# A hybrid decoder trunk on one core: another order of the seven products in the w_up blocks, and a first tile that is loaded beside its weights

## The chip, the cores and the metric

The kernel runs on one core of one Trainium2 chip. The metric is device time in microseconds (us) of one execution, as the median over runs; smaller is better. TensorE (PE) multiplies, VectorE (DVE), ScalarE (ACT) and GpSimd (POOL) work elementwise, and SyncE (SP) issues most of the loads.

## The reference, cut to what matters

The computation is a decoder trunk of two layers on 512 tokens of width 1024. Each layer is a mixer (attention and a Mamba-2 scan side by side) and a SwiGLU feed-forward, each behind an RMSNorm and added to the residual. What the change touches is the first input projection and the feed-forward:

```python
D_MODEL, SEQ, DEPTH = 1024, 512, 2
FFN_HIDDEN = ((8 * D_MODEL + 3 * 256 - 1) // (3 * 256)) * 256    # 2816

def rmsnorm(x, w):
    y = x * lax.rsqrt(jnp.mean(x * x, axis=-1, keepdims=True) + EPS)
    return y * w

def swiglu(h, w_gate, w_up, w_down):
    return (jax.nn.silu(h @ w_gate) * (h @ w_up)) @ w_down

def reference(x, ...):
    h = x
    for layer in range(DEPTH):
        h = h + hybrid_mixer(rmsnorm(h, norm_mix[layer]), w_in[layer], ...)   # begins with h @ w_in
        h = h + swiglu(rmsnorm(h, norm_ffn[layer]), w_gate[layer], w_up[layer], w_down[layer])
    return rmsnorm(h, final_norm)
```

Everything is float32. The kernel reaches that precision with three products for each: an operand is split into a rounded high part and the rest (`xh` and `xl` of an activation, `whi` and `wlo` of a weight), and `whi·xh + whi·xl + wlo·xh` is accumulated.

## The kernel before, in words

**Recording and order.** The code does not issue instructions directly. Each helper (`act`, `copy`, `tt`, `stt`, `mms`, `load`) records an operation with a cost, the tiles it reads and writes, and a priority that the last `at(...)` set; a list scheduler (`plan.schedule`) then simulates the recorded program and fixes the order of instructions on each engine. On the chip every engine works strictly in that order: an instruction that waits holds up all that stand behind it on its engine. Since helpers issue everything, almost all rows of the trace carry the line of a helper (L459 is every product, L444 `copy`, L446 `act`, L407 `tt`, L418 `stt`, L463 `load`), and an operation is known by its tiles.

**Weights.** A chunk of weights (1 MB, 256 columns wide) is loaded into `raw` (two buffers) by the SP queue. ACT casts a block of 128 columns to `whi`, DVE subtracts to get `wlo`. Both have three buffers (`NWH`), handed out in rotation: a split can begin only when the products of the third split before it are done.

**Start.** The transposed input lies in eight tiles `hT[0..7]` of 128x512, the first four blocks of `w_in` in eight tiles `raw0[0..7]` (`w` in the trace). SP loads `pmix` (norm weights), then `hT[0]`, `raw0[0]`, `hT[1]`, and so on. Meanwhile PE multiplies `ones` by itself nine times (18 instructions). For each k the loop at L592 splits `hT[k]` (ACT `xh`, DVE `xl`) and `raw0[k]` (ACT CAST `xh<-w`, DVE `xl<-w`), issues 12 products into four accumulators, and squares `hT[k]` on ACT for the norm. Behind these 96 products PE forms column sums of squares (`tr<-ones,sq`), and transposes the rotary tables (`ropetok`) and the reciprocal root (`rcol`), whose copy `rstd` scales the four accumulators (`cu`).

**Feed-forward.** The hidden width is done in parts of 6, 6, 6 and 4 blocks of 128 columns. In parts 1 to 3 each pair of blocks has two plain products for `w_gate` (512 columns an instruction, "gate1" and "gate2" below), and for `w_up` the function `seven()`: a seven-product (Strassen-like) form of the 2x2 block product, with instructions of 256 columns. There are 8 such pairs a layer, 16 in all. They are numbered 0 to 15 here, #0 to #7 in layer 0. `seven` splits four operands: `a` (the raw first block), `b` and `c` (sums of quarters of the block, formed by four DVE additions into one tile `wsum`), and `d` (one raw quarter). Its products stand in the code in the order a, a, b, b, c, c, d; `p17`, `p26`, `p45` and `p3` are their accumulators, `e`, `m` and `o` what DVE makes of them. The products of gate1 and gate2 are interleaved with each other and with the neighbouring pairs' products by the scheduler. Each part ends with the `w_down` blocks ("down").

Of the kernel before, what the change touches and what calls it, by code (L numbers as in the profile page):

```python
# [15 lines left out]
ALU = mybir.AluOpType  # L16
# [163 lines left out]
class VTile:  # L180


    def __init__(self, pool, shape, dtype, tag, name, space):
        self.pool, self.shape, self.dtype, self.tag, self.name = pool, shape, dtype, tag, name
        self.psum = space
        self.ap = None
        self.writer, self.readers, self.uses = None, [], 0
        self.live = False

    def get(self):  # L190
        if self.ap is None:
            kw = {} if self.tag is None else {"tag": self.tag[0], "bufs": self.tag[1]}
            self.ap = self.pool.tile(self.shape, self.dtype, name=self.name, **kw)
        return self.ap


class Op:
# [6 lines left out]
class Plan:  # L204
# [4 lines left out]
    def add(self, eng, dur, outs, ins, fn, prio=None, table=None, lat=0.0):  # L209
        o = Op()  # L210
        o.eng, o.dur, o.lat, o.fn, o.table = eng, dur, lat, fn, table
        o.prio = self.t if prio is None else prio
        o.n, o.users = len(self.ops), []
        deps = set()
        outs = [v.tile for v in outs]
        ins = [v.tile for v in ins if isinstance(v, View)]
        for t in ins:
            assert t.writer is not None, f"{t.name} is read before it is written"
            deps.add(t.writer)
        for t in outs:  # L220
            if t.writer is not None:
                deps.add(t.writer)
            deps.update(t.readers)
        for t in ins:
            t.readers.append(o)
        for t in outs:
            t.writer, t.readers = o, []
        deps.discard(o)
        o.tiles = list({id(t): t for t in outs + ins}.values())
        for t in o.tiles:  # L230
            t.uses += 1
        o.deps = deps
        for d in deps:
            d.users.append(o)
        self.ops.append(o)
        return o
# [107 lines left out]
def hybrid_trunk(  # L344
# [24 lines left out]
    def C(shape, name, dt=F32):  # L369
        n = nm(name)  # L370
        return View(VTile(cp, shape, dt, None, n, False), shape)

    def G(name, dt=F32):
        return new(gp, [P, S], dt, ("g", NG), name)
# [16 lines left out]
    def R(v):  # L391
        return v.real() if isinstance(v, View) else v

    def at(t):
        plan.t = t
# [30 lines left out]
    def memset(eng, o, val):  # L426
        plan.add(eng, 0.1 + 0.9e-3 * o.free, [o], [], lambda: ENG[eng].memset(R(o), val))

    TABLE = {AF.Exp: "exp", AF.Ln: "ln", AF.Silu: "silu", AF.Sin: "silu"}

    def act(o, a, func, scale=None, bias=None, accum=None):
        ptr = [s for s in (scale, bias) if isinstance(s, View)]
        outs = [o] + ([accum] if accum is not None else [])

        def fn():
            kw = {}
            if scale is not None:
                kw["scale"] = R(scale)
            if bias is not None:
                kw["bias"] = R(bias)  # L440
            if accum is not None:
                kw["accum_out"] = R(accum)
            if func == AF.Copy and not kw:
                nc.scalar.copy(R(o), R(a))  # L444
            else:
                nc.scalar.activation(R(o), R(a), func, **kw)  # L446
        cost = 0.83e-3 * o.free + (0.053 if a.tile.psum else 0.093) + 0.093 * len(ptr)
        plan.add("act", cost, outs, [a] + ptr, fn, table=TABLE.get(func))

    def mms(outs, prods, each, prio=None):  # L450

# [7 lines left out]
                    nc.tensor.matmul(R(p[0]), R(p[1]), R(p[2]), start=p[3], stop=p[4])  # L459
        plan.add("pe", each * len(prods), outs, ins, fn, prio, lat=0.08)  # L460

    def load(o, src, kb):
        plan.add("sp", max(0.47, kb / 351.0), [o], [], lambda: nc.sync.dma_start(R(o), src), lat=2.0)  # L463

    def tposes(t, parts, name=None):
        mms([t], parts, 0.108)


    at(-40.0)
    pmix = C([P, 16], "pmix")  # L470
    load(pmix, columns[:, PC_MIX:PC_MIX + 16], 8)
    hT = [C([P, S], f"hT{k}") for k in range(KD)]

    raw0 = []
    for k in range(KD):
        load(hT[k], xT[k * P:(k + 1) * P, :], 256)
        raw0.append(G("w0"))
        load(raw0[k], w_in[0, k * P:(k + 1) * P, XBC_COL + 1024:XBC_COL + 1024 + S], 256)
    at(-35.0)
    ones = C([P, P], "ones")  # L480
    memset("pool", ones, 1.0)

    t = tr()
    mms([t], [(t[:, 0:P], ones, ones, True, True)] * 9, 0.43)
    nhalf = C([P, NT], "nhalf")
    memset("pool", nhalf, -0.5)

# [63 lines left out]
    class Norm:  # L551
# [2 lines left out]
        def __init__(self, n):  # L554
            self.n, self.ss, self.row = n, None, None

        def square(self, tl, eng="dve"):
            s = G("sq")
            act(s, tl, AF.Square)
            if self.ss is None:  # L560
                self.ss = s
            else:
                tt(eng, self.ss, self.ss, s, ALU.add)
# [31 lines left out]
    for k in range(KD):  # L595
        at(-20.0 + k)
        xs_next.append(split_x(hT[k], pmix[:, k:k + 1]))
        wh, wl = split_x(raw0[k], None)
        for j, t in enumerate(first):
            js = slice(j * P, (j + 1) * P)  # L600
            xh, xl = xs_next[k]
            mms([t], [(t, wh[:, js], xh, k == 0, False), (t, wh[:, js], xl, False, False),
                      (t, wl[:, js], xh, False, k == KD - 1)], 0.2165, clock[0])
            clock[0] += 3 * 0.2165
        at(-12.0 + k)
        norm_next.square(hT[k])


    at(-12.0)
# [504 lines left out]
    def seven(ids, X):  # L1114
# [4 lines left out]
        def split(src, nk=KD):  # L1119
# [2 lines left out]
            tt("dve", lo[:, 0:nk, :], src, hi[:, 0:nk, :].bitcast(F32), ALU.subtract)  # L1122
            return hi, lo
        a = split(raw[:, :, 0:P])
        sm = big("wsum").rearrange("p (k c) -> p k c", c=P)
        s = [sm[:, i * KQ:(i + 1) * KQ, :] for i in range(4)]
        tt("dve", s[0], q[1][0], q[1][1], ALU.add)
        tt("dve", s[1], s[0], q[0][0], ALU.add)
        tt("dve", s[2], q[0][0], q[1][0], ALU.add)
        tt("dve", s[3], q[0][1], s[1], ALU.add)  # L1130
        b = split(sm[:, 0:KD, :])
        c = split(sm[:, KD:, :])
        d = split(q[1][1], KQ)
        t1_, t2_ = slice(0, HH), slice(HH, S)

        def prod(o, w, k0, xs, half):
# [15 lines left out]
            return v.rearrange("p (u c) -> p u c", u=2)  # L1152

        b1, b2 = X["b"][0:KQ], X["b"][KQ:]
        p17, p26 = hold(), acc()
        e, m, o = G("e"), G("m"), G("o")
        prod(p17[:, 0:HH], a, 0, b1, t1_)
        copy("act", e[:, 0:HH], p17[:, 0:HH])
        prod(p26[:, 0:HH], a, KQ, b2, t1_)
        prod(p26[:, HH:], b, KQ, X["t12"], t2_)  # L1160
        tt("dve", halves(m), halves(p26), bcast(e[:, 0:HH]), ALU.add)
        p45, p3 = acc(), tr()
        prod(p45[:, HH:], b, 0, X["t12"], t1_)
        prod(p17[:, HH:], c, 0, X["t34"], t1_)
        tt("dve", e[:, HH:], p17[:, HH:], m[:, HH:], ALU.add)
        prod(p3[:, 0:HH], c, KQ, b2, t2_)
        tt("dve", m[:, HH:], m[:, HH:], p3[:, 0:HH], ALU.add)
        tt("dve", m[:, HH:], m[:, HH:], p45[:, HH:], ALU.add)
        prod(p45[:, 0:HH], d, 0, X["t34"], t2_)
        tt("dve", halves(o), halves(p45), bcast(e[:, HH:]), ALU.add)  # L1170
        at(clock[0] - 4.0)
        return m, o

# [100 lines left out]
```

## Time and profile before

| what | value |
|---|---|
| median of 3 runs | 1323.34 us (1321.87, 1323.34, 1323.98) |
| profiled execution | 1324.0 us, of which the span of the trace is 1322.2 us |
| busy share | PE 98%, PE's weight loads 81%, DVE 68%, ACT 49%, POOL 11% |
| mean granted clock of TensorE | 0.995 |
| busiest group of the page | `acc<-xh,whi` products, 588.4 us in 1552 instructions |
| loads | 115.57 MB, mean 87 GB/s |

PE's busy time is 1294.6 us of the 1322.2 us span. A duration of a product in the trace is longer than its spacing to the next, since products are pipelined; an instruction of 512 columns is printed with 0.39 us and one of 256 columns with 0.28 us. Time lost on PE shows in three ways: as idle time in brackets behind a row, as a larger distance between the starts of two rows, or as a longer printed duration.

### The profile page before, as it was taken

The page shows a single profiled execution, that of the slowest core. Times are in us where ns is not written, and L with a number is a line of the kernel's source. Part 1 is how long each engine was busy: PE and PEld are TensorE (multiplying, and loading weights), DVE is VectorE, ACT ScalarE, POOL GpSimd, SP SyncE. Part 2 cuts the span into 40 slices and gives each one's busy share as a digit, 9 for nine tenths or more (in the row PEclk, how much of TensorE's full clock was granted, in tenths as well). Part 3 has the DMA queues.
Part 4 walks back from the last instruction along what each step waited for, and adds up shares of the span by engine and source line. Part 5 has one row for each costly group of instructions (what it writes and reads, how often), then busy time and mean ns, then how long its engine had stood idle before and what let it go on. Part 6 is the DMA issues. An engine that isn't in the chain of part 4 may idle for free.

```text
span 1322.2 us, 17020 instructions
## 1 busy us (share of the span) xinstructions
PE 1294.6 (98%) x6674; PEld 1067.4 (81%) x6674; DVE 905.7 (68%) x1510; ACT 653.0 (49%) x1029; POOL 140.2 (11%) x109
## 2 busy tenths in 40 slices
PE   8999998999999999999999999999999999999997
PEld 7877776778888888888888777767888889888896
DVE  6987779768746555555779687887786456465464
ACT  7677656656323323323647687466553233243253
POOL 0014455000000000000000234620000000000000
PEclk9999999999999999999999999999999999999999
DMA  7222211123232233233332222111332332322421
GB/s 242 64 64 64 64 65 64 33 80 102 90 112 96 69 123 99 78 112 96 96 98 65 94 66 65 56 40 45 88 112 84 119 96 72 120 96 73 135 96 63
DMA packets 105727, 115.57 MB, mean 87 GB/s; under 512 B 4656, under 2 KB 95024, under 8 KB 105648
## 3 DMA queue, kind: packets, MB, share of 16 engines
q1 hardware_dynamic: 105648, 114.49, 27.4%
q8 instruction: 52, 0.85, 0.3%
q14 instruction: 27, 0.22, 0.1%
HBM read 112.39 MB, written 2.10 MB: 87 GB/s over the span
## 4 chain that ended last, share of the span: by engine, by line
PE 87%; DVE 7%; ACT 2%; POOL 2%; issue 1%; DMA 0%; POOLq 0%; SPq 0%; DVEq 0%; ACTq 0%
PE acc L459 72%; PE hold L459 7%; PE tr L459 6%; PE tr L457 3%; DVE wlo L407 2%; DVE qs L407 1%; POOL xbc L407 1%; DVE xbc L418 1%; POOL qr L407 1%; ACT whi L444 1%; DVE wsum L407 0%; DVE qs L921 0%; POOL qs L407 0%; ACT L446 0%; DVE sa L413 0%
## 5 line engine op out<-in xcount | busy, mean ns | idle before, releaser
L459 PE MATMUL acc<-xh,whi 128*128 128x512 f32 (+1 forms) x1552 | 588.4, 379 | 1.4 <-DVE o L407 0.9
L459 PE MATMUL acc<-xl,whi 128*128 128x512 f32 (+1 forms) x1552 | 579.4, 373 | 0.0
L459 PE MATMUL acc<-xh,wlo 128*128 128x512 f32 (+1 forms) x1536 | 573.3, 373 | 4.2 <-DVE wlo L407 4.2
L444 ACT CAST whi<-raw 128x1024 fp32r<-128x1024 f32 (+3 forms) x248 | 212.4, 859 | 335.2 <-PE acc L459 303.0
L459 PEld LDWEIGHTS acc<-xh,whi 128*128 128x128 f32 x1552 | 293.2, 189 | 55.1 <-issue 5.6
L459 PEld LDWEIGHTS acc<-xh,wlo 128*128 128x128 f32 x1536 | 289.7, 189 | 58.6 <-DVE wlo L407 6.7
L459 PEld LDWEIGHTS acc<-xl,whi 128*128 128x128 f32 x1552 | 293.3, 189 | 47.1 <-issue 0.5
L407 DVE TENSOR_TENSOR wlo<-raw,whi 128x1024 fp32r<-128x1024 f32 (+2 forms) x240 | 246.8, 1030 | 27.6 <-ACT whi L444 27.3
L407 DVE TENSOR_TENSOR hT<-hT,acc 128x512 f32<-128x512 f32 x104 | 71.1, 685 | 103.6 <-PE acc L459 102.9
L407 DVE TENSOR_TENSOR wlo<-wsum,whi 128x1024 fp32r<-128x1024 f32 x32 | 39.0, 1224 | 88.4 <-ACT whi L444 88.4
L573 POOL TENSOR_TENSOR rcol<-var,nhalf 128x4 f32<-128x4 f32 x8 | 8.7, 1089 | 577.2 <-DVE var L413 577.2
L446 ACT ACT_TABLE_LOAD x49 | 62.9, 1283 | 6.6 <-DMA hT<-in_xT_dram 4.1
L444 ACT CAST whi<-wsum 128x1024 fp32r<-128x1024 f32 x32 | 33.5, 1048 | 53.9 <-PE acc L459 46.3
L418 DVE SCALAR_TENSOR_TENSOR xbc<-cu,prm,xbc 128x511 f32<-128x511 f32 (+2 forms) x72 | 58.4, 819 | 0.8
L444 ACT CAST xh<-ga 128x512 fp32r<-128x512 f32 x44 | 27.3, 621 | 54.5 <-DVE ga L407 38.6
L446 ACT ACTIVATE sa<-sa,mx 128x512 f32<-128x512 f32 (+3 forms) x64 | 36.0, 562 | 36.5 <-DVE mx L979 36.2
L1230 POOL TENSOR_TENSOR fr<-fvar,nhalf 128x1 f32<-128x1 f32 x4 | 2.2, 546 | 353.5 <-DVE fvar L413 353.5
L979 DVE CUSTOM_DVE_ANT_0 sa<-tr,cst 128x512 f32<-128x512 f32 (+3 forms) x64 | 30.7, 479 | 10.3 <-PE tr L459 10.2
L459 PE MATMUL hold<-xh,wlo 128*128 128x256 f32 x128 | 36.3, 284 | 0.0
L459 PE MATMUL hold<-xl,whi 128*128 128x256 f32 x128 | 36.2, 283 | 0.0
L459 PE MATMUL hold<-xh,whi 128*128 128x256 f32 x128 | 36.1, 282 | 0.0
L407 DVE TENSOR_TENSOR xl<-ga,xh 128x512 fp32r<-128x512 f32 x44 | 30.3, 688 | 8.3 <-ACT xh L444 8.2
(216 smaller groups left out, 1654.8 us busy)
## 6 DMA issues: line engine op xcount, KB each, us to landing
raw<-in_w_in_dram SPq DMA_DIRECT2D x24, 1024.0 KB, 5.1
raw<-in_w_gate_dram SPq DMA_DIRECT2D x22, 1024.0 KB, 5.2
raw<-in_w_up_dram SPq DMA_DIRECT2D x22, 1024.0 KB, 5.2
raw<-in_w_down_dram SPq DMA_DIRECT2D x24, 768.0 KB, 4.5
raw<-in_w_out_dram SPq DMA_DIRECT2D x8, 1024.0 KB, 5.0
raw<-in_w_out_dram SPq DMA_DIRECT2D x8, 512.0 KB, 6.3
hT<-in_xT_dram SPq DMA_DIRECT2D x8, 256.0 KB, 5.3
w<-in_w_in_dram SPq DMA_DIRECT2D x8, 256.0 KB, 5.4
```

Source lines behind the costliest of these rows:

```text
L407: lambda: ENG[eng].tensor_tensor(R(o), R(a), R(b), alu))
L418: lambda: nc.vector.scalar_tensor_tensor(R(o), R(a), R(s), R(b), op0, op1))
L444: nc.scalar.copy(R(o), R(a))
L446: nc.scalar.activation(R(o), R(a), func, **kw)
L457: nc.tensor.transpose(R(p[0]), R(p[1]), R(p[2]))
L459: nc.tensor.matmul(R(p[0]), R(p[1]), R(p[2]), start=p[3], stop=p[4])
L573: lambda: nc.gpsimd.tensor_tensor(R(self.r), R(v), R(nhalf), ALU.pow))
L979: nc.vector.tensor_tensor_reduce(R(sa[:, 0:nk]), R(t[:, 0:nk]), R(cst[:, C_MASK + S - nk:C_MASK + S]), 1.0, 3e38, ALU.add, ALU.min, R(m))
L1230: lambda r=r, v=v: nc.gpsimd.tensor_tensor(R(r), R(v), R(nhalf[:, 0:1]), ALU.pow))
```

## The change

There are two parts, in different places of the program.

**In `seven`:** the split of `d` is recorded right behind that of `a`, ahead of the sums; the sum tile is seen as two halves (`Part`), so that the split of `b` depends on the first two sums alone and stands ahead of the last two; the products come in the order a, a, d, b, b, c, c. The additions that read `p45` (into `o` and `m`) now stand ahead of the last product of `c`.

**At the start:** `hT[0]` is loaded first and `pmix` behind it; `raw0[0]` is loaded from ACT's queue; a one-column ACTIVATE on `ones` is recorded before the first split, ten products of `ones` are issued for nine, and the square of `hT[k]` is recorded behind the loop and made to wait for the split of `hT[k+3]`.

```diff
+class Part:
+    def __init__(self, view):
+        self.view, self.root = view, view.tile
+        self.pool, self.tag, self.name, self.psum = None, None, view.tile.name, view.tile.psum
+        self.writer, self.readers = None, []
...
-    def act(o, a, func, scale=None, bias=None, accum=None):
+    def act(o, a, func, scale=None, bias=None, accum=None, after=()):
...
-        plan.add("act", cost, outs, [a] + ptr, fn, table=TABLE.get(func))
+        plan.add("act", cost, outs, [a] + ptr + list(after), fn, table=TABLE.get(func))
...
-    def load(o, src, kb):
-        plan.add("sp", max(0.47, kb / 351.0), [o], [], lambda: nc.sync.dma_start(R(o), src), lat=2.0)
+    def load(o, src, kb, eng="sp"):
+        plan.add(eng, max(0.47, kb / 351.0), [o], [], lambda: ENG[eng].dma_start(R(o), src), lat=2.0)
...
     at(-40.0)
+    ones = C([P, P], "ones")
+    memset("pool", ones, 1.0)
     pmix = C([P, 16], "pmix")
-    load(pmix, columns[:, PC_MIX:PC_MIX + 16], 8)
...
         load(hT[k], xT[k * P:(k + 1) * P, :], 256)
+        if k == 0:
+            load(pmix, columns[:, PC_MIX:PC_MIX + 16], 8)
         raw0.append(G("w0"))
-        load(raw0[k], w_in[0, k * P:(k + 1) * P, XBC_COL + 1024:XBC_COL + 1024 + S], 256)
+        load(raw0[k], w_in[0, k * P:(k + 1) * P, XBC_COL + 1024:XBC_COL + 1024 + S], 256, "sp" if k else "act")
+
+    warm = small([P, 1], "warm", 1)
+    act(warm, ones[:, 0:1], AF.Square)
...
-    mms([t], [(t[:, 0:P], ones, ones, True, True)] * 9, 0.43)
+    mms([t], [(t[:, 0:P], ones, ones, True, True)] * 10, 0.43)
...
+    for k in range(KD):
         at(-12.0 + k)
-        norm_next.square(hT[k])
+        norm_next.square(hT[k], after=[xs_next[min(k + 3, KD - 1)][0]])
...
         a = split(raw[:, :, 0:P])
+        d = split(q[1][1], KQ)
         sm = big("wsum").rearrange("p (k c) -> p k c", c=P)
-        s = [sm[:, i * KQ:(i + 1) * KQ, :] for i in range(4)]
+        sums = [part(sm[:, 0:KD, :]), part(sm[:, KD:, :])]
+        s = [sums[i // 2][:, i % 2 * KQ:(i % 2 + 1) * KQ, :] for i in range(4)]
         tt("dve", s[0], q[1][0], q[1][1], ALU.add)
         tt("dve", s[1], s[0], q[0][0], ALU.add)
+        b = split(sums[0])
         tt("dve", s[2], q[0][0], q[1][0], ALU.add)
         tt("dve", s[3], q[0][1], s[1], ALU.add)
-        b = split(sm[:, 0:KD, :])
-        c = split(sm[:, KD:, :])
-        d = split(q[1][1], KQ)
+        c = split(sums[1])
...
         prod(p26[:, 0:HH], a, KQ, b2, t1_)
+        prod(p45[:, 0:HH], d, 0, X["t34"], t2_)
         prod(p26[:, HH:], b, KQ, X["t12"], t2_)
         tt("dve", halves(m), halves(p26), bcast(e[:, 0:HH]), ALU.add)
-        p45, p3 = acc(), tr()
         prod(p45[:, HH:], b, 0, X["t12"], t1_)
         prod(p17[:, HH:], c, 0, X["t34"], t1_)
         tt("dve", e[:, HH:], p17[:, HH:], m[:, HH:], ALU.add)
+        tt("dve", halves(o), halves(p45), bcast(e[:, HH:]), ALU.add)
+        tt("dve", m[:, HH:], m[:, HH:], p45[:, HH:], ALU.add)
         prod(p3[:, 0:HH], c, KQ, b2, t2_)
         tt("dve", m[:, HH:], m[:, HH:], p3[:, 0:HH], ALU.add)
-        tt("dve", m[:, HH:], m[:, HH:], p45[:, HH:], ALU.add)
-        prod(p45[:, 0:HH], d, 0, X["t34"], t2_)
-        tt("dve", halves(o), halves(p45), bcast(e[:, HH:]), ALU.add)
```

Since the scheduler decides, the order on the engines is shown at two places. A name is followed by a number for its buffer. The first place is the start of ACT's program; `xh<-hT,pmix` is the split of an input tile, `xh<-w` that of a weight tile. Before:

```order
L446 ACT_TABLE_LOAD
L446 ACTIVATE xh_102<-hT_2_90,pmix_72 128x512
L446 ACTIVATE sq_106<-hT_2_90 128x512
L444 CAST xh_112<-w_10_92 128x512
L446 ACTIVATE xh_116<-hT_3_98,pmix_72 128x512
L444 CAST xh_120<-w_11_100 128x512
L446 ACTIVATE sq_130<-hT_3_98 128x512
```

And with the change:

```order
L480 DMA w_11_76<-in_w_in_dram 128x512
L463 ACT_TABLE_LOAD
L463 ACTIVATE warm_95<-ones_72 128x1
L461 CAST xh_107<-w_11_76 128x512
L463 ACTIVATE xh_109<-hT_3_74,pmix_93 128x512
L463 ACTIVATE xh_115<-hT_4_97,pmix_93 128x512
L461 CAST xh_123<-w_12_103 128x512
```

The table load has moved ahead of the first instruction that needs loaded data, the weight's cast ahead of the input's, and the first square behind three more input tiles (it is the eleventh row of the change, outside this piece).

The second place is DVE in pair #9 (layer 1). Here `wlo<-wsum` are the splits of `b` and `c` (in this order), the 128x512 `wlo<-raw` is that of `d`, `wlo<-raw` of 128x1024 is gate1 of the next pair, and the `wsum` that is written anew is that of the next pair. Before:

```order
L407 TENSOR_TENSOR wlo_9259<-raw_9136,whi_9255 128x512
L407 TENSOR_TENSOR wsum_9305<-raw_9261 128x512
L407 TENSOR_TENSOR wlo_9309<-wsum_9208,whi_9297 128x1024
L407 TENSOR_TENSOR wlo_9313<-wsum_9208,whi_9311 128x1024
L407 TENSOR_TENSOR wsum_9305<-wsum_9305,raw_9261 128x512
L407 TENSOR_TENSOR wsum_9305<-raw_9261 128x512
L407 TENSOR_TENSOR m_9342<-acc_9290,e_9288 128x512
L407 TENSOR_TENSOR wsum_9305<-raw_9261,wsum_9305 128x512
L407 TENSOR_TENSOR wlo_9360<-raw_9204,whi_9350 128x1024
```

And with the change:

```order
L424 TENSOR_TENSOR wlo_9274<-raw_9070,whi_9270 128x512
L424 TENSOR_TENSOR wlo_9296<-wsum_9115,whi_9285 128x1024
L424 TENSOR_TENSOR wlo_9327<-wsum_9115,whi_9319 128x1024
L424 TENSOR_TENSOR wsum_9343<-raw_9276 128x512 x2
L424 TENSOR_TENSOR wlo_9352<-raw_9198,whi_9341 128x1024
L424 TENSOR_TENSOR m_9366<-acc_9287,e_9310 128x512
L424 TENSOR_TENSOR wsum_9343<-wsum_9343,raw_9276 128x512
L424 TENSOR_TENSOR e_9310<-hold_9278,m_9366 128x256
L424 TENSOR_TENSOR wlo_9385<-raw_9198,whi_9374 128x1024
```

The next pair's first sum has moved from a place ahead of `wlo` of `b` to one behind `wlo` of `c`; two sums now stand right ahead of gate1's `wlo`.

Counted over the program, the order of splits before is a, b, c, d in 11 pairs and a, d, b, c in five (#1, #4, #7, #9, #12): there the scheduler had put `d`'s split ahead. `b` then takes the buffer of gate2, in the other pairs that of gate1. With the change all 16 pairs have a, d, b, c, with `d` in gate1's buffer, `b` in gate2's and `c` in that of `a`. The counts of instructions on PE, DVE and ACT are the same but for the warm-up and its ACTIVATE.

## Rows read from the trace of the kernel before

**Rows 1.** Waits of PE, whole span: waits for, us in total, times, longest.

```profile
PE acc L459 <- ACT xh L444: 2.5, 1, 2.5
```

**Rows 2.** Waits of PE, 395 to 662 us, layer 0's feed-forward.

```profile
PE acc L459 <- DVE wlo L407: 1.7, 3, 0.6
PE acc L459 <- DVE o L407: 0.9, 1, 0.9
PE acc L459 <- DVE m L407: 0.4, 1, 0.4
```

**Rows 3.** Waits of PE, 1040 us to the end, layer 1's feed-forward.

```profile
PE acc L459 <- DVE wlo L407: 2.5, 2, 1.3
```

**Rows 4.** Timeline, 0 to 12 us: start, duration, instruction, in brackets idle before it.

```profile
0.73 0.38 SPq L463 DMA_DIRECT2D pmix<-in_columns_dram  x1
0.99 3.73 PE L459 MATMUL tr<-ones 128*128 128x128 f32 x18 [0.99 <-POOL nhalf L427]
1.18 0.42 SPq L463 DMA_DIRECT2D hT<-in_xT_dram  x1
1.64 0.42 SPq L463 DMA_DIRECT2D w<-in_w_in_dram  x1
...
4.11 1.28 ACT L446 ACT_TABLE_LOAD   x1 [4.11 <-DMA hT<-in_xT_dram]
5.41 0.72 ACT L446 ACTIVATE xh<-hT,pmix 128x512 fp32r<-128x512 f32 x1
6.16 0.75 DVE L418 SCALAR_TENSOR_TENSOR xl<-hT,pmix,xh 128x512 fp32r<-128x512 f32 x1 [6.16 <-ACT xh L446]
6.56 0.60 ACT L444 CAST xh<-w 128x512 fp32r<-128x512 f32 x1
7.21 0.57 PE L459 MATMUL acc<-xh,xh 128*128 128x512 f32 x1 [2.49 <-ACT xh L444]
...
11.70 0.39 PE L459 MATMUL acc<-xh,xh 128*128 128x512 f32 x1
```

**Rows 5.** Windows of 1 us: busy share by engine, granted clock, DMA share, GB/s.

```profile
3.00:4.00 1.00, 1.00 (x7) 1.00 (x6) 0.00 (x0) 0.00 (x0) 0.00 (x0) 1.00 0.99 358
8.00:9.00 1.00, 1.00 (x4) 0.81 (x4) 1.00 (x2) 1.00 (x3) 0.00 (x0) 0.50 1.01 373
```

**Rows 6.** Timeline, 28 to 35 us.

```profile
29.18 0.80 DVE L424 COPY ropetok<-rope 128x32 f32<-128x32 f32 x8
...
30.74 0.95 PE L459 MATMUL tr<-ones,sq 128*128 128x1 f32 x8
...
31.55 1.07 PE L457 MATMUL tr<-ident,ropetok 128*128 128x128 f32 x8
...
34.64 0.69 DVE L407 TENSOR_TENSOR cu<-acc,rstd 128x512 f32<-128x512 f32 x1 [2.76 <-ACT rstd L444]
```

**Rows 7.** Timeline, 628 to 631 us, pair #7 behind gate2.

```profile
628.37 0.28 PE L459 MATMUL acc<-xh,whi 128*128 128x256 f32 x1
628.40 1.05 ACT L444 CAST whi<-wsum 128x1024 fp32r<-128x1024 f32 x1 [0.84 <-PE acc L459]
...
629.48 1.23 DVE L407 TENSOR_TENSOR wlo<-wsum,whi 128x1024 fp32r<-128x1024 f32 x1 [5.30 <-ACT whi L444]
...
629.92 0.28 PE L459 MATMUL acc<-xl,whi 128*128 128x256 f32 x1
...
630.76 0.39 PE L459 MATMUL acc<-xh,wlo 128*128 128x256 f32 x1 [0.56 <-DVE wlo L407]
```

**Rows 8.** Timeline, 1086 to 1089 us, pair #9.

```profile
1087.05 0.69 DVE L407 TENSOR_TENSOR wsum<-raw 128x512 f32<-128x512 f32 x1 [5.44 <-DMA raw<-in_w_up_dram]
```

**Rows 9.** Timeline, 441.5 to 444.2 us, pair #1's end.

```profile
443.44 0.42 DVE L407 TENSOR_TENSOR m<-m,acc 128x256 f32<-128x256 f32 x1
...
443.92 0.39 PE L459 MATMUL acc<-xh,whi 128*128 128x256 f32 x1 [0.41 <-DVE m L407]
```

**Rows 10.** The page's part on DMA issues: count, KB each, us to landing.

```profile
raw<-in_w_up_dram SPq DMA_DIRECT2D x22, 1024.0 KB, 5.2
```

More of the change, by code (lines that the diff above doesn't have):

```diff
@@ L186, in __init__ @@
         self.ap = None
+        self.root = self
         self.writer, self.readers, self.uses = None, [], 0
@@ L194, in get, with part @@
         return self.ap
+class Part:
[3 more added lines that the diff above has]
+        self.writer, self.readers = None, []
+    def get(self):
+        return self.view.real()
+def part(view):
+    return View(Part(view), view.shape)
 class Op:
@@ L228, in add @@
         deps.discard(o)
-        o.tiles = list({id(t): t for t in outs + ins}.values())
+        o.tiles = list({id(t.root): t.root for t in outs + ins}.values())
         for t in o.tiles:
@@ L476, in hybrid_trunk @@
         load(hT[k], xT[k * P:(k + 1) * P, :], 256)
+        if k == 0:
+            load(pmix, columns[:, PC_MIX:PC_MIX + 16], 8)
         raw0.append(G("w0"))
-        load(raw0[k], w_in[0, k * P:(k + 1) * P, XBC_COL + 1024:XBC_COL + 1024 + S], 256)
+        load(raw0[k], w_in[0, k * P:(k + 1) * P, XBC_COL + 1024:XBC_COL + 1024 + S], 256, "sp" if k else "act")
+    warm = small([P, 1], "warm", 1)
+    act(warm, ones[:, 0:1], AF.Square)
     at(-35.0)
-    ones = C([P, P], "ones")
-    memset("pool", ones, 1.0)
     t = tr()
-    mms([t], [(t[:, 0:P], ones, ones, True, True)] * 9, 0.43)
+    mms([t], [(t[:, 0:P], ones, ones, True, True)] * 10, 0.43)
     nhalf = C([P, NT], "nhalf")
@@ L555, in __init__, with square @@
             self.n, self.ss, self.row = n, None, None
-        def square(self, tl, eng="dve"):
+        def square(self, tl, eng="dve", after=()):
             s = G("sq")
-            act(s, tl, AF.Square)
+            act(s, tl, AF.Square, after=after)
             if self.ss is None:
@@ L1154, in seven @@
         b1, b2 = X["b"][0:KQ], X["b"][KQ:]
-        p17, p26 = hold(), acc()
+        p17, p26, p45, p3 = hold(), acc(), acc(), tr()
         e, m, o = G("e"), G("m"), G("o")
```

## The prediction, as it was put on record before the change was run

> **What bounds the kernel now.** I began with the page's busy shares: PE works 98% of the span, so time can only be won where PE stands still, or where it works at a lower clock. Next I read the list of PE's waits over the whole span for what the change touches at the start, and there is one entry: 2.5 us for ACT's `xh` [rows 1]. The same list, cut to the feed-forward stretches, gives the waits that belong to `seven`: three waits for `wlo` of 1.7 us together, one of 0.9 for `o` and one of 0.4 for `m` in layer 0 [rows 2], and two waits for `wlo` of 2.5 us together in layer 1 [rows 3]. All else that PE waits for (attention, norms, the scan) is in stretches whose order the change leaves as it was. Then I read each place in the timeline.
>
> At the start [rows 4] the reader should see a chain. The first input tile is issued at 1.18 us, behind `pmix`. ACT's first instruction is the table load, and it begins at 4.11, when that tile has landed: 2.93 us after its issue. Then follow, one behind the other on ACT, the load (1.28), `xh` of the input, its square, and the cast of the weights; PE's first product starts at 7.21. The warm-up products had ended at 4.72 (0.99 + 3.73), hence the 2.49 us idle. And PE then runs slow: the granted clock is 1.00 in the window at 3 us, and 0.50 (1.2 of 2.4 GHz) in the one at 8 us, behind that idle time [rows 5].
>
> In the feed-forward, pair #7 stands for all five `wlo` waits [rows 7]. ACT begins to cast `b` at 628.40, when gate2 has given its buffer back; DVE's `wlo` ends at 630.71 (629.48 + 1.23). From 628.37 to 629.92 PE makes 13 steps of 0.119 us with what it has, and then wants `b`'s low part. These five are just the pairs in which `d`'s split stands ahead of `b`'s. In the two of layer 1 there is more: DVE's additions for the *next* pair stand ahead of `b`'s `wlo`, and wait for a load until 1087.05 [rows 8], so that `wlo` starts late although its cast is done.
>
> **The start, step by step.** `hT[0]` takes `pmix`'s place in the queue: 0.73 for 1.18. Landing 2.93 us later, as before, it would be there at 3.66. The weight tile now starts beside it instead of 0.46 us behind. In the window at 3 us the engines move 358 GB/s with a DMA share of 0.99 [rows 5], so 256 KB take 0.73 us of all engines' time; if the two tiles interleave, both land up to 0.73 later, at 4.39. I take 4.15 for both, between these, and 3.66 and 4.39 as bounds. The Trainium skill speaks against this edit here (DMA: Bandwidth & Descriptors, "Issuing engines are not separate DMA queues"): loads of different issuers run on the same 16 engines and interleave, so that only issue time is saved. By that alone the landing would be the late bound; the trace, with one queue, cannot show it.
>
> Behind the landing only the cast (0.60) and `xh` of the input (0.72) are left on ACT, since the table load and the square are gone from in between, and PE starts 0.05 behind the last of them, as it did (6.56 + 0.60 to 7.21): 4.15 + 0.60 + 0.72 + 0.05 = 5.5, less a little overlap of rows that follow each other on ACT, 5.4 (4.9 to 5.7). The saved load counts 1.30 us, from its row to the start of the next (4.11 to 5.41) [rows 4]. The Trainium skill (ScalarE: Activation LUTs, "What ACT_TABLE_LOAD costs") gives 1.28 us for the load, with which the row agrees, and 1.38 more for a drain, which the next row's start doesn't show; with it the gain here would be 1.4 us larger. `pmix` (8 KB) is now issued behind `hT[0]` and is wanted by the same `xh`; it is small, and I cost it at nothing while the weight tile lands behind it.
>
> PE's second product needs DVE's `xl` of the input, which starts when `xh` is done and takes 0.75, where a product at full clock takes 0.23: a wait of 0.55. Before it cost nothing, as the square and cast stood in between. The first k took 4.49 us for its 12 products (7.21 to 11.70), though the other 84, from 11.70 to 30.74, came every 0.227: 1.77 lost. Now the ten warm-ups end at 5.13 (0.99 + 10 x 3.73 / 9), 0.3 us before the first product, and I take the clock as staying full: 12 x 0.227 + 0.55 = 3.3. So the 96 products end at 5.4 + 3.3 + 84 x 0.227 = 27.8 rather than 30.74: 2.9 earlier. ACT keeps pace: one `xh`, one square and one cast took 5.41 to 7.16, 1.75 us per k, against 2.72 on PE, and 512 KB per k take 1.46.
>
> What is late next is `ropetok`. DVE's eight copies end at 29.98 and PE transposes at 31.55 [rows 6]; moved 2.9 earlier PE would be there at 28.65. The sines and what leads to them hang on DVE and ACT, which also start the loop earlier and have lost its squares, so they come forward too, but I charge 0.2 here. If they don't come forward at all, PE waits until 29.98 and the gain is 1.55. Behind this the norm's column leads to `rstd`, for which DVE now waits 2.76 before `cu` [rows 6]; DVE is the busier engine from there on, so its earlier start is carried through. **Term A: 2.7 to 2.9, taken as 2.8; bounds 1.5 and 3.5** (early landing).
>
> **The products, step by step.** Two things change for `b`. It stands behind `a` and `d`, so between gate2's last product and `b`'s first there are now at least 24 products of 256 columns, where the five pairs had 12 (counted in the order of all 16 pairs): 24 x 0.119 = 2.86, and its low part is wanted 0.24 later, at 3.1. It is ready 2.34 us after gate2's end (628.37 to 630.71), so the wait goes, with 0.76 to spare. And the next pair's sums have left the place ahead of it. `c` in `a`'s buffer has 3.7 us between, and each gate 4.4 or more, against the same 2.4. `d` is half as large.
>
> What the waits cost is more than their list says: 4.2 idle; each waiting row is reached 0.16 late in the list, as the row before it is printed with 0.28 at a spacing of 0.119 (five times: 0.8); and the restarted row lasts 0.39 for 0.28 (0.5). That is 5.5. The `m` wait, where a product waits until DVE has added `p45` into `m` behind all else of the pair [rows 9], costs 0.4 + 0.16 + 0.1 = 0.67, and goes, since that addition is now ahead of `c`'s last 12 products. The `o` wait of 0.9 stays as another: after layer 0's last pair `down` needs gate1's product with `m`, which then ends last, about as late. **Term B: 6.2; bounds 3.5** (half of the `wlo` time comes back as shorter waits) **and 6.9** (the `o` wait goes too).
>
> The extra warm-up and one-column ACTIVATE cost nothing, as PE and ACT wait for the first tile there.
>
> **The sum.** 2.8 + 6.2 = 9.0. The profiled execution took 1324.0 (span 1322.2 and 1.8 around it), 0.7 above the median of 1323.34; I subtract from the median: 1314.3.
>
> **The rivals.**
> *The wait moves on.* `c` and the next gate's split stand behind `b` on ACT and DVE, and what PE no longer waits for there it waits for one split later. For it: DVE and ACT work in fixed order, and the five pairs show DVE idle over 5 us and then two `wlo` at a stretch. Against: 3.7 us and more of cover. Half of term B would be left: 1323.3 - 2.8 - 3 = 1317.5.
> *The start is absorbed.* The clock stays at half behind the change of stretch, or the rotary tables and `rstd` don't come forward. For it: 0.50 in the window at 8 us, and 0.3 us of idle is left; the transposes' bound above. Term A would be some 0.5 to 1.5: 1316.4.
> *Slower.* DVE's two sums of the next pair now stand right ahead of gate1's `wlo`. Their load takes 5.2 us [rows 10], can be issued when `d`'s split and the sums have freed `raw`, and lands some 5.5 us behind gate2's end; with 1.3 us of sums and 1.2 of `wlo` gate1 is ready at 8.1. It is wanted after 78 products, at 9.3: 1.2 to spare. The point that decides is a landing later than 6.7 behind gate2's end; at 7.8 it would cost over 1 us in each of 16 pairs, more than the 9.0 gained and 2.6 besides: 1326 or more. For it: the head-of-line wait of 5.44 on just such a row before [rows 8].
> *It doesn't do what it says.* The waits are for something else that is late by as much, and the start is set by the loads: 1323.
>
> **Chances.** As forecast 0.62; the wait moves on 0.14; the start absorbed 0.15; slower 0.04; nothing 0.05. About 0.2% (2.6 us) is what a measurement of this kernel tells from no change. The first three are all faster by more, less 0.01 where both rivals fall together: faster 0.90, same 0.06, slower 0.04. The forecast's own range, by its bounds and the runs' spread of 2.1 us, is 1311 to 1316.5. The range reaches to the first two rivals: 1310.5 to 1318.5.
>
> **What would show it.** At the start: the table load before 3 us, the first product at 5.4, granted clock 1.00 at 8 us, `tr<-ones,sq` at 27.8, `cu` nearly 3 us earlier. In the feed-forward: no waits for `wlo` or `m` in the list, one wait of about 1 us left ahead of layer 0's `down`. Wrong would be: waits for `whi` or `wlo` at other products, a first product behind 6 us, idle time of PE ahead of `ropetok` above half a microsecond, or gate products that wait for `wlo<-raw` behind a `wsum` that waits for a DMA.

## The result and the profile after

The changed kernel takes 1314.09 us (median of 5 runs, 1314.0 to 1317.89); the kernel before took 1323.98 us in the five runs beside it (1321.87 to 1327.02). The ratio is 0.9931 (95% interval 0.9909 to 0.9952): 9 us faster, where 1314.3 had been forecast. The profiled execution took 1314.08, its span is 1312.1. The total is right, but its two terms are not: in the traces the start gave less and the products more.

These are the waits of PE ahead of products into `acc`, over the whole span, from the view of [rows 1 to 3] (waits for, us in total, times, longest):

```profile
PE acc L476 <- ACT xh L463: 0.7, 1, 0.7
PE acc L476 <- DVE xl L435: 0.3, 1, 0.3
PE acc L476 <- DVE xl L424: 0.2, 1, 0.2
```

That is all of them. No wait for `wlo`, `m` or `o` is left; the 2.5 us of the start are 0.7, and 0.3 behind it. The third row stands at 637.09 us, in layer 0's last `down`: where the wait for `o` stood, PE now waits for the low part of `down`'s own operand `ga`:

```profile
637.09 0.50 PE L476 MATMUL acc<-xl,whi 128*128 128x512 f32 x1 [0.23 <-DVE xl L424]
```

The start in the timeline of the changed kernel answers to [rows 4]:

```profile
0.73 0.40 ACTq L480 DMA_DIRECT2D w<-in_w_in_dram  x1
...
0.73 0.38 SPq L480 DMA_DIRECT2D hT<-in_xT_dram  x1
...
0.99 4.25 PE L476 MATMUL tr<-ones 128*128 128x128 f32 x20 [0.99 <-POOL nhalf L444]
1.17 1.28 ACT L463 ACT_TABLE_LOAD   x1 [1.17 <-PEq L1279]
...
4.62 0.62 ACT L461 CAST xh<-w 128x512 fp32r<-128x512 f32 x1 [1.96 <-DMA w<-in_w_in_dram]
...
5.15 1.33 ACT L463 ACTIVATE xh<-hT,pmix 128x512 fp32r<-128x512 f32 x2
...
5.92 0.50 PE L476 MATMUL acc<-xh,xh 128*128 128x512 f32 x1 [0.68 <-ACT xh L463]
...
6.71 0.50 PE L476 MATMUL acc<-xl,xh 128*128 128x512 f32 x1 [0.28 <-DVE xl L435]
7.04 0.39 PE L476 MATMUL acc<-xh,xl 128*128 128x512 f32 x1
```

The table load has gone to 1.17, and PE's second product waits for `xl` as foreseen. But the first weight tile lands at 4.62, behind the late bound of 4.39, and the first product follows at 5.92. The window at 8 us answers to the second of [rows 5]: full clock.

```profile
8.00:9.00 1.00, 1.00 (x6) 0.84 (x5) 1.00 (x2) 0.95 (x3) 0.00 (x0) 1.00 1.05 365
```

Behind the first 96 products, for [rows 6]:

```profile
28.35 0.95 PE L476 MATMUL tr<-ones,sq 128*128 128x1 f32 x8
28.42 0.35 ACT L463 ACTIVATE rope<-rope 128x32 f32<-128x32 f32 x2
...
29.33 0.16 DVE L430 TENSOR_SCALAR var<-tr 128x4 f32<-128x4 f32 x1 [0.47 <-PE tr L476]
29.41 0.81 DVE L441 COPY ropetok<-rope 128x32 f32<-128x32 f32 x8
...
30.23 1.06 PE L474 MATMUL tr<-ident,ropetok 128*128 128x128 f32 x8
...
32.49 1.29 DVE L424 TENSOR_TENSOR cu<-acc,rstd 128x512 f32<-128x512 f32 x2 [2.28 <-ACT rstd L461]
```

The products end 2.39 us earlier, the transposes of the rotary tables only 1.32. The sines (`rope<-rope` on ACT) come 0.31 earlier (28.42 for 28.73), but `var<-tr`, which waits for PE's sums of squares, now stands ahead of the copies into `ropetok` on DVE. So these come later than before (29.41 for 29.18), and PE transposes when the last is done (30.22). `cu` is 2.15 earlier.

In pair #9 the reader should look at DVE behind gate2, for [rows 8]:

```profile
1079.06 1.23 DVE L424 TENSOR_TENSOR wlo<-wsum,whi 128x1024 fp32r<-128x1024 f32 x1 [1.10 <-ACT whi L461]
1082.03 1.23 DVE L424 TENSOR_TENSOR wlo<-wsum,whi 128x1024 fp32r<-128x1024 f32 x1 [1.75 <-ACT whi L461]
1083.53 1.29 DVE L424 TENSOR_TENSOR wsum<-raw 128x512 f32<-128x512 f32 x2 [0.27 <-DMA raw<-in_w_up_dram]
1084.74 1.22 DVE L424 TENSOR_TENSOR wlo<-raw,whi 128x1024 fp32r<-128x1024 f32 x1
```

Both `wlo` of the pair are done before the next pair's load lands at 1083.53; gate1's `wlo` ends at 1085.96. PE uses it here:

```profile
1087.77 0.39 PE L476 MATMUL acc<-xh,wlo 128*128 128x512 f32 x1
```

So the place at which it could have become slower has 1.8 us to spare.

Pair #8 is not like this, alone among the 16: there the next pair's first sum stands ahead of `wlo` of `b` in the changed kernel, and did not before. It waits for the load:

```profile
1059.38 0.69 DVE L424 TENSOR_TENSOR wsum<-raw 128x512 f32<-128x512 f32 x1 [5.21 <-DMA raw<-in_w_up_dram]
1059.98 1.22 DVE L424 TENSOR_TENSOR wlo<-wsum,whi 128x1024 fp32r<-128x1024 f32 x1
...
1061.52 0.28 PE L476 MATMUL acc<-xh,wlo 128*128 128x256 f32 x1
```

`wlo` is done at 1061.20 and PE uses it at 1061.52. There is no wait, but only because the load landed 5.2 us behind its issue; a load that is 0.3 us slower brings one.

**Where the time went.** Looking up the same instructions in both traces gives the time by stage. "Start" ends where DVE's fourth `qr<-acc,rstd` of layer 0 begins (189.64 us before); the feed-forward stages run between ACT's `rstd<-tr` copies (the fourth, fifth and eighth: 312.21, 673.52 and 964.05 before) and the end of the span (1322.2). Each number is the stage's time in the kernel less that stage's before, in us, from one trace of each kernel; the kernels of the experiments are included.

| kernel | first product at | 96 products done | start | layer 0 attention, output | feed-forward 0 | layer 1 mixer | feed-forward 1, end | span |
|---|---|---|---|---|---|---|---|---|
| before | 7.21 | 30.74 | 0 | 0 | 0 | 0 | 0 | 1322.2 |
| changed | 5.92 | 28.35 | -2.34 | +0.45 | -4.37 | +0.03 | -3.88 | 1312.1 |
| e1_start_only | 5.84 | 28.28 | -2.44 | +0.16 | -0.32 | +4.19 | +0.25 | 1324.1 |
| e2_seven_only | 7.08 | 30.67 | +0.03 | -0.31 | -4.41 | +2.69 | -3.91 | 1316.3 |
| e5_order_only | 5.81 | 28.29 | -2.39 | +0.35 | -4.38 | +4.34 | -3.73 | 1316.4 |
| e6_halves_only | 5.97 | 28.43 | -2.27 | -0.33 | -2.00 | +4.04 | -2.92 | 1318.7 |
| e3_w0_on_sp | 6.07 | 28.23 | -1.31 | +2.72 | -4.36 | +4.36 | -3.76 | 1319.9 |
| e4_no_warm | 5.88 | 28.33 | -2.45 | +2.69 | -4.38 | +4.36 | -3.76 | 1318.7 |
| e8_squares_early | 5.82 | 28.27 | -2.62 | +0.01 | -4.39 | +1.20 | -3.88 | 1312.5 |
| e9_w0_halves | 5.26 | 27.72 | -3.00 | +0.15 | -4.38 | +0.07 | -3.63 | 1311.4 |
| e10_halves_and_fill | 5.18 | 27.65 | -3.12 | +1.10 | -4.42 | +1.11 | -2.53 | 1314.4 |
| e11_change_and_fill | 5.82 | 28.29 | -2.42 | +1.09 | -4.42 | +3.00 | -2.94 | 1316.5 |
| e12_change_again | 5.85 | 30.16 | -0.52 | -0.30 | -4.42 | +2.70 | -3.65 | 1316.0 |

The two columns of the mixers belong to stretches that the change leaves alone. They differ by up to 4 us between the traces; what that is stands at the end. Each experiment below is therefore judged by its stage, and its ratio to runs of the kernel before, made with it, is given beside. In the runs of e1, e2, e5 and e6 the kernel before took 1326.89 us, of e3, e4, e8 and e9 1327.39, of e10 to e12 1324.36; the expectations count from 1324.

### The profile page after: what moved, and what is told of

It reads as the page before. It is cut to its first block, busy times and chain, and to the rows that moved or that the text cites. A ratio compares the mean times of both kernels' runs of the same rounds, so it can differ in the third digit from the quotient of the medians.

```text
span 1312.1 us, 17056 instructions
## 1 busy us (share of the span) xinstructions
PE 1292.0 (98%) x6676; PEld 1068.0 (81%) x6676; DVE 898.3 (68%) x1510; ACT 651.8 (50%) x1030; POOL 141.1 (11%) x109
## 4 chain that ended last, share of the span: by engine, by line
PE 89%; DVE 6%; POOL 2%; ACT 2%; issue 1%; DMA 0%; POOLq 0%; ACTq 0%; DVEq 0%
PE acc L476 73%; PE hold L476 7%; PE tr L476 6%; PE tr L474 3%; DVE wlo L424 1%; DVE qs L424 1%; POOL xbc L424 1%; POOL qr L424 1%; DVE xbc L435 1%; DVE qs L943 0%; DMA w<-in_w_in_dram 0%; DVE sa L430 0%; DVE sa L1001 0%; DVE qr L424 0%; POOL qs L424 0%
## 5 line engine op out<-in xcount | busy, mean ns | idle before, releaser
L1001 DVE CUSTOM_DVE_ANT_0 sa<-tr,cst 128x512 f32<-128x512 f32 (+3 forms) x64 | 30.6, 477 | 10.3 <-PE tr L476 10.1
```

The costliest lines, as they stand in the source:

```text
L1001: nc.vector.tensor_tensor_reduce(R(sa[:, 0:nk]), R(t[:, 0:nk]), R(cst[:, C_MASK + S - nk:C_MASK + S]), 1.0, 3e38, ALU.add, ALU.min, R(m))
```

## The experiments

**The two parts by themselves.** e1 takes the changed kernel with `seven` as before; e2 takes it with the start as before.

```diff
# e1: seven() of the kernel before
-        prod(p45[:, 0:HH], d, 0, X["t34"], t2_)      # third
         prod(p26[:, HH:], b, KQ, X["t12"], t2_)
...
+        prod(p45[:, 0:HH], d, 0, X["t34"], t2_)      # last, with the splits and sums of before
# e2: start of the kernel before (pmix first, w on SP, no warm ACTIVATE, nine products, squares in the loop)
```

> Only the start is changed; seven() is as before. By the shift read from the trace after the change (2.4 us at the end of the first 96 products, 1.9 left from 210 us on): 1322 us beside 1324, the five waits for wlo and the m wait still there with 4.6 us of idle time, first product at 5.9. Rival, the start is absorbed further down: no later event than 100 us comes earlier by over 0.5 us, 1324.

> Only seven() is changed; the start is as before. If the two parts add up: 8.2 us faster than before, 4.3 of it in layer 0's feed-forward and 3.9 in layer 1's, no wait for wlo, 1315.8 beside 1324. As the prediction's term had it: 6.2 faster, 1317.8. Rival, the wait moves on when the stretch ahead isn't shifted: 1319 to 1321, with waits for another whi or wlo.

e1: ratio 0.9974 (0.9963 to 0.9985), 1321.75 us beside 1326.89. The list of PE's waits in e1 has all five for `wlo` back:

```profile
PE acc L476 <- DVE wlo L424: 4.3, 5, 1.4
PE acc L476 <- DVE o L424: 0.9, 1, 0.9
```

The start gives 2.44 and the feed-forward almost nothing (0.32 in layer 0, where the wait for `m` is gone against the expectation, though `seven` is as before). e2: 0.9939 (0.9923 to 0.9954), 1318.19; 4.41 and 3.91 from the feed-forward, 8.3 together, and no wait for `wlo`. The stages add up: 2.4 and 8.3 apart, 2.3 and 8.25 together. The time of e2 lies nearer to the 1317.8 of the smaller term, but it is 8.7 us below the 1326.89 of the kernel before beside it; by that and by the stages the larger one holds. Neither rival is seen.

**The two edits in `seven` by themselves.** Both keep the changed start.

```diff
# e5: one dependency for the whole sum tile, b's split behind all four sums
-        sums = [part(sm[:, 0:KD, :]), part(sm[:, KD:, :])]
+        sums = [sm[:, 0:KD, :], sm[:, KD:, :]]
...
-        b = split(sums[0])
         tt("dve", s[2], q[0][0], q[1][0], ALU.add)
         tt("dve", s[3], q[0][1], s[1], ALU.add)
+        b = split(sums[0])
# e6: halves of the sums, but products and d's split in the order of before
+        sums = [part(sm[:, 0:KD, :]), part(sm[:, KD:, :])]
```

> The changed kernel without the halves of the sums: b's split waits for all four sums again; the product order a, a, d, b, b, c, c stays. If the products put ahead of b are what counts: 1314 as with both, no wait for wlo. Rival, the earlier split of b counts: two more sums (0.69 us each) ahead of b's wlo bring back waits of up to 1.4 us in the pairs where the load comes late, 1316 to 1320.

> The changed kernel with the halves of the sums but the product order a, a, b, b, c, c, d of before. If the products put ahead of b are what counts: at least half of the feed-forward's gain is lost, waits for wlo in layer 0 and 1 of 2 us or more, 1317 to 1320. Rival, the halves count, since they let b be split ahead of d in all 16 pairs: waits for wlo under 0.5 us, 1314 to 1316.

e5: 0.9936 (0.9916 to 0.9956), with -4.38 and -3.73 where both edits gave -4.37 and -3.88, and no wait for `wlo`. The halves add nothing that shows; the time, 1318.20, lies in the rival's range, but 8.7 us below the kernel before beside it. e6: 0.9955 (0.9941 to 0.997), -2.00 and -2.92. PE's waits for DVE in e6's feed-forward:

```profile
PE acc L476 <- DVE m L424: 1.0, 1, 1.0
PE acc L476 <- DVE o L424: 0.9, 1, 0.9
```

Here the expectation of the first theory failed, though the time, 1319.82, lies in its range: no wait for `wlo` is left, and less than half of the gain is lost. With the halves the scheduler puts `b`'s split ahead of `d`'s in the five pairs too, and their waits are gone. What the halves don't do is shorten the pair's end: the waits for `m` in pairs #1 and #4 are gone, but one of 1.0 stands at the end of pair #7, and `o` stays. So either edit removes the five waits; the order of products removes most of the rest too, 3.3 us more in all.

**The start, edit by edit.**

```diff
# e3: first weight tile on SP's queue
-        load(raw0[k], ..., 256, "sp" if k else "act")
+        load(raw0[k], ..., 256)
# e4: no ACTIVATE ahead of the landing
-    warm = small([P, 1], "warm", 1)
-    act(warm, ones[:, 0:1], AF.Square)
# e8: squares in the loop again
+        norm_next.square(hT[k])
```

> The changed kernel with the first weight tile on SP's queue again, behind the first input tile and pmix (issue at 1.6 us for 0.7). If the transfer engines set the landing, and the other queue only saves issue time: the weight tile lands at 4.6 to 5.1, the first product starts 0 to 0.5 us later than the 5.9 of the changed kernel. Rival, the second queue brings bandwidth of its own: 0.9 us later or more.

> The changed kernel without the one-column ACTIVATE. If the table load waits with the instruction behind it, as it did before: it begins at 4.6 when the weights land, the first product starts 1.3 us later, at 7.2, behind an idle time of 2 us, and PE runs at half clock behind it as before (1 us more): 96 products end 1.3 to 2.4 us later than with the change. Rival, the load is issued ahead of that wait anyway: no difference.

> The changed kernel with the squares recorded in the loop as before, with no wait for a later split. The square of the first tile then stands ahead of the second tile's split on ACT (0.6 us). If ACT has that much room in each k (1.75 us of work in 2.72): 96 products end within 0.2 us of the changed kernel. Rival, the first steps have none: 0.3 to 0.7 us later, waits for xh or xl at the second k.

e3: 0.9927 (0.99 to 0.9954). Its timeline at the start:

```profile
1.64 0.42 SPq L480 DMA_DIRECT2D w<-in_w_in_dram  x1
...
3.73 0.72 ACT L463 ACTIVATE xh<-hT,pmix 128x512 fp32r<-128x512 f32 x1 [1.50 <-DMA pmix<-in_columns_dram]
...
5.40 0.62 ACT L461 CAST xh<-w 128x512 fp32r<-128x512 f32 x1 [0.95 <-DMA w<-in_w_in_dram]
...
6.07 0.50 PE L476 MATMUL acc<-xh,xh 128*128 128x512 f32 x1 [0.95 <-ACT xh L461]
```

With less beside them, the input and `pmix` are there at 3.73, and the weights are there at 5.40, 0.8 later than on the second queue and later than the 4.6 to 5.1 expected; since ACT has then already split the input, the first product is only 0.15 later and the 96 products end at the same time. So the second queue lands its tile earlier by no more than it was issued earlier (1.64 for 0.73). The Trainium skill says as much (DMA: Bandwidth & Descriptors, "Issuing engines are not separate DMA queues": loads of different issuers share the same engines, and only issue time is saved), and the trace agrees with it. Yet the start loses 1.0 against the changed kernel (-1.31 for -2.34), at a place that the expectation does not name. The last three tiles of the loop are issued 1.2 to 1.5 us later on SP, and so is what follows them (`prm` at 11.15 for 10.00). ACT and DVE, which show no idle time from 13 us to the sines in either trace, are behind by as much (`posf<-posi` on DVE at 19.91 for 18.45, the sines' table load on ACT at 28.45 for 27.13), so the `ropetok` copies are late (e3's timeline at 30 us):

```profile
30.19 0.80 DVE L441 COPY ropetok<-rope 128x32 f32<-128x32 f32 x8
31.01 1.07 PE L474 MATMUL tr<-ident,ropetok 128*128 128x128 f32 x8
```

That is what the second queue is worth in this trace: 1 us, at the rotary tables, by the loads that stand behind it on SP's queue. Why they fall behind by more than the one load's issue (0.47) is shown in part only: in the window from 3 to 4 us, with less in flight, the engines move 177 GB/s in e3 and 385 in the changed kernel.

e4: 0.9949 (0.9931 to 0.9967), but the start is the same as with the change (-2.45), and so the rival is right (e4's timeline):

```profile
1.16 1.28 ACT L461 ACT_TABLE_LOAD   x1 [1.16 <-PEq L1277]
...
4.58 0.62 ACT L461 CAST xh<-w 128x512 fp32r<-128x512 f32 x1 [2.14 <-DMA w<-in_w_in_dram]
```

The load runs ahead of the cast's wait without help. Before, it began only when the input had landed [rows 4]; there the instruction behind it was the ACTIVATE that reads the input and `pmix`, here it is a cast that reads one tile. Which of the two differences decides was not tried. e8: 0.9918 (0.989 to 0.9946); 96 products end 0.08 earlier than with the change, the start is 0.28 better. Delaying the squares brings nothing that shows.

**A start that is shorter still.** The first weight tile comes in two halves of 256 columns on ACT's queue; DVE rounds the first while ACT splits the input; nine warm-up products.

```diff
+            for u in range(2):
+                load(raw0[0][u][:, 0:HH], w_in[0, 0:P, c0:c0 + HH], 128, "act")
...
+                    copy("dve", hi[:, 0:HH], raw0[0][u][:, 0:HH])      # u == 0; ACT for u == 1
```

> The changed kernel with the first weight tile loaded in two halves of 256 columns, both on ACT's queue, the first half rounded on DVE beside ACT's split of the input; nine warm-up products. If landing (bandwidth shared by what is in flight) and the two steps in a row on ACT set the first product: it starts at 5.1 for 5.9, 96 products end 0.6 to 0.9 us earlier, and the time falls by as much. Rival, the landing has a fixed time and is not a matter of bytes: the first product starts 0.5 earlier at most, by the cast alone.

In e9's timeline:

```profile
4.25 0.29 DVE L441 CAST xh<-w 128x256 fp32r<-128x256 f32 x1 [4.25 <-DMA w<-in_w_in_dram]
4.49 0.72 ACT L463 ACTIVATE xh<-hT,pmix 128x512 fp32r<-128x512 f32 x1 [1.34 <-DMA pmix<-in_columns_dram]
...
5.26 0.50 PE L476 MATMUL acc<-xh,xh 128*128 128x512 f32 x1 [0.62 <-ACT xh L463]
```

The half lands at 4.25, the first product is 0.66 earlier, the 96 products end 0.63 earlier, and the start gains 0.66: as expected in size, and more than the 0.5 of the rival. What bounds it now is `pmix`, at 4.49. The ratio is 0.9914 (0.9887 to 0.994), which lies a little below that of the changed kernel, but the intervals overlap: the gain is seen in the stage, not in the time.

**The half clock in the mixer.** Both kernels run at half clock for some us when the attention scores begin in each layer, behind waits of PE. e10 (on e9) and e11 (on the change) fill one of these waits.

```diff
             mms([t], [(t[:, i:i + 1], self.ss[:, i * P:(i + 1) * P], ones[:, 0:1], True, True) for i in range(NT)]
+                + [(t[:, P:2 * P], ones, ones, True, True)] * extra, 0.45)
...
-            nrm.spread()
+            nrm.spread(3 * g)
```

> The kernel with the first weight tile in halves, and three products of ones by ones more behind the sums of squares of the second gated norm in each layer, where PE stands idle for 1.3 us before the attention scores. If that idle time is what brings PE to half clock there: granted clock 1.00 from 206 to 213 us and at the same place in layer 1, 1.7 us earlier behind each of the two or more, 1309 to 1311, and a smaller spread between runs. Rival, the half clock comes anyway, by the other waits around it (1.05 before, 0.7 behind): the same as without, 1313 to 1317.

> The changed kernel with the same three products of ones in each layer, and the first weight tile loaded whole. By the same theory: 1310 to 1312; rival: 1314 to 1318.

> The changed kernel once more, beside the two others on the same chip: 1314 to 1317; by its trace again 8.2 us from the feed-forward, whatever the half-clock stretches at the attention's start do.

e10: 0.994 (0.9926 to 0.9954), e11: 0.9952 (0.994 to 0.9965), e12: 0.9934 (0.9919 to 0.995), beside each other on one chip. The wait that was filled is shorter (0.54, and 1.31 in the changed kernel), but another stands behind it, and the half clock comes. In e10's timeline, and its window at 208 us:

```profile
205.95 0.47 PE L476 MATMUL tr<-kh,qs 128*128 128x512 f32 x1 [0.54 <-DVE mx L1021]
207.82 0.76 PE L476 MATMUL tr<-kh,qs 128*128 128x512 f32 x1 [1.17 <-ACT qs L461]
```

```profile
208.00:209.00 1.00, 1.00 (x3) 0.81 (x4) 0.99 (x2) 0.64 (x2) 0.00 (x0) 0.50 0.00 0
```

The rival holds (e11, at 1318.74, lies even above its range); the scheduler had also moved scores around the three products, so the wait alone was not taken away, and filling all waits there was not tried.

Both also give less in layer 1's feed-forward (2.53 and 2.94), and that is pair #8. The load there landed 6.6 us behind its issue in e10 and 6.3 in e11, the next pair's sum waits for it, and one wait for `wlo` is back, of 1.0 in e10 and 0.7 in e11. In e10's timeline:

```profile
1061.73 0.69 DVE L424 TENSOR_TENSOR wsum<-raw 128x512 f32<-128x512 f32 x1 [6.66 <-DMA raw<-in_w_up_dram]
...
1063.62 0.39 PE L476 MATMUL acc<-xh,wlo 128*128 128x256 f32 x1 [1.04 <-DVE wlo L424]
```

Why these two loads were slow was not found. e12 repeats the feed-forward's gain (-4.42, -3.65).

## Why the prediction came out right, step by step

**What bounds the kernel: right.** Time came from PE's standing still and from the clock at the start, at the places that were named. The feed-forward's part has nearly the same size in the traces of the eight kernels with the new order and no fill: 4.36 to 4.42 and 3.63 to 3.91.

**Term A, 2.8 forecast, 2.34 measured at the end of its stage, 1.9 behind layer 0's attention.** Table load and square are off the path, the wait for `xl` is there (the second product 0.79 behind the first; 0.23 without), and the clock was full at 8 us. The step that missed is the landing: 4.62 instead of 4.15, out of the bounds even; it makes 0.5. The bounds took the cost of the two tiles side by side as the 0.73 us of one tile at the full rate, from the landing before; in e3, where the input tile comes ahead of the weights, it and `pmix` are there at 3.73. `pmix` and the next input tile were under way too; how much each adds was not isolated. That `ropetok` comes next was right. That the sines come forward was right by 0.3 us only, and the copies behind them come later than before; but PE has other products in its order to do before the transposes, and only 0.24 of the 2.39 is lost between the 96 products and `cu`. The other 0.45 were lost to a half-clock stretch at the attention's start; that stage differs by as much and more between the kernels with this start or nearly this start (-0.33 to +2.72).

The clock needed luck as well. The 1.00 at 3 us of [rows 5] is no reading: the trace before has its first record of the clock at 4.1 us, and up to a first record the view prints 1.00. Row by row, the warm-up products stand 0.21 us apart up to there and 0.11 behind it, so PE was at half speed at 3 us. In the changed kernel the first record, of full clock, is at 4.7 us, ahead of the first product; in four of the other ten kernels with a changed start (e4, e6, e8, e10) it is at 5.9 to 6.3, behind it, and in e12 at 10.6. The ten warm-up products do not ensure it.

**Term B, 6.2 forecast, 8.25 measured, above its upper bound of 6.9** (7.1 by its own terms, 6.2 and the 0.9 of `o`). The mechanism is the one that was forecast: `b` has cover, and no wait moves on to `c` or a gate. That the next pair's sums have left the place ahead of `b` is true of pairs #9 and #12, but in pair #8 one has come there. It cost nothing in the changed kernel's trace, and in e10 and e11 about 1 us. The term was undersized, because I took it from the list of waits. From the starts of all of PE's rows in the two traces, steps that are longer than the median of their kind by over 0.06 us come to 9.2 us before and 1.7 after in the two feed-forward stretches: 7.5 less. To the five waits (5.5) and `m` (0.67) they add a second wait for `m` in pair #4 that no list shows (0.33). Before:

```profile
540.50 0.39 PE L459 MATMUL acc<-xh,wlo 128*128 128x512 f32 x1
540.96 0.39 PE L459 MATMUL acc<-xh,whi 128*128 128x256 f32 x1
```

The wait for `o` became a shorter one (1.3 before, 1.0 after), and restarts of 0.07 to 0.11 us at the handover between blocks and at the end come to 0.7 less. The other 0.8 is mostly in steps of 512 columns that are longer by about 0.01, 194 before and 105 after; no run isolates their cause.

**The sum.** The spans differ by 10.1 us and the profiled executions by 9.9, where 9.0 had been added up: the errors of the terms have opposite signs (-0.9 behind layer 0's attention, and +2.05) and leave 1.1. That the time itself came out within 0.2 us is luck: the median that I subtracted from lay 0.7 below the profiled execution, which takes up most of the rest, and the same kernel has a median of 1316.9 in the runs of e12 (1314.28 to 1318.03).

**The rivals.** The wait did not move on to a later split in any trace; what came back in e10 and e11 is a wait for `b` itself, behind a late load. The start was absorbed in part, and e12 shows how much it can be: there the same program ran its first products at half speed, and the start gained 0.52. The slower rival's mechanism exists (DVE waits 0.27 for the load, ahead of gate1's `wlo`), with more slack than the 1.2 estimated: 1.8.

**What I had put down to the wrong edit.** The one-column ACTIVATE isn't needed (e4), nor are the late squares (e8), nor the halves of the sums (e5), once the rest is there. The second queue, which I had as a matter of landing, earns 1 us in the one trace of e3, by what stands behind it on SP's queue.

## What to carry to other kernels

A wait's price is the difference between the starts of the two rows around it, less the usual step; a list of idle times leaves out late starts, slow restarts and waits that are shorter than a pipelined row. When a split waits for a rotating buffer, put work that needs neither that buffer nor its successor between the last reader and the first use; count it in steps, and look at what stands in front of it on the engine that fills the buffer, in every block and not at one: the order of pair #9 was not that of pair #8. A load that is moved to another queue can be worth more by what it frees on the queue that it leaves than by its own landing: follow that queue to its last load.

## What the runs showed of the hardware that was not expected

The half clock at the attention's start comes in every profile, but its length differs between executions of the same work: in layer 0 PE was at 0.50 from 207 to 212 us in the changed kernel,

```profile
207.00:212.00 5.00, 4.93 (x13) 3.44 (x13) 4.90 (x14) 3.00 (x7) 1.43 (x2) 0.50 0.00 0
```

and in e3, with the same instructions there and the same waits ahead (1.05 and 1.32), for ten:

```profile
209.00:219.00 10.00, 8.30 (x24) 5.97 (x23) 9.13 (x18) 4.37 (x9) 6.07 (x5) 0.51 0.00 0
```

That is the +2.72 of the table. In e3 the half clock begins over 2 us later behind the same waits, and a third wait of PE, of 1.02 us for `rcol` (0.07 in the changed kernel), falls inside the stretch; whether that is why it lasts longer was not tried. In layer 1 the same place accounts for most of the +2.7 to +4.4; in e1, e3, e4, e5, e6, e8 and e11 a second stretch, at 781 to 786 us, adds to it. The feed-forward of the kernels without the fill repeats to 0.3 us meanwhile. Most of the spread of 4 us between a kernel's runs can come from these stretches, though only one trace of each kernel was read; and a ratio between two kernels needs the stage beside it. What sets their length was not found.

In e12 the first products stood 0.43 us apart, as in the window of half clock before [rows 5], while the granted clock of that window reads 1.00. The trace of e12 has no record of the clock ahead of 10.6 us, and behind it the products stand 0.23 apart: before a trace's first record the column shows nothing. The 20 warm-up products of e12 also took 4.63 us, where they took 4.25 in the changed kernel. Why the clock rose so late there was not found. The warm-up, the window and PE's rows in e12:

```profile
0.99 4.63 PE L476 MATMUL tr<-ones 128*128 128x128 f32 x20 [0.99 <-POOL nhalf L444]
```

```profile
8.00:9.00 1.00, 1.00 (x4) 0.72 (x3) 1.00 (x2) 0.97 (x3) 0.00 (x0) 1.00 1.07 379
```

```profile
7.23 0.63 PE L476 MATMUL acc<-xh,xl 128*128 128x512 f32 x1
7.66 0.63 PE L476 MATMUL acc<-xh,xh 128*128 128x512 f32 x1
8.09 0.63 PE L476 MATMUL acc<-xl,xh 128*128 128x512 f32 x1
```
